# Gate projections as seven half-size products, with the latents and q put ahead of the attention loop

## The chip, the cores and the metric

The kernel runs on one core of a Trainium2 chip. The metric is the device time of one execution in microseconds (us). The time before is the median of three runs. A profile of one execution shows which engine ran which instruction when: PE (TensorE, matmuls; PEld its weight loads), DVE (VectorE), ACT (ScalarE), POOL (GpSimd), and SP, whose queue issues DMAs. Each engine works through its instructions in the order in which the program holds them, and waits there for what the next one needs.

## What is computed

One decoder block for 1024 rows of 1024 fp32 values, with two attentions side by side whose outputs are gated and added, and a SwiGLU:

```python
h = rmsnorm(x, mix_norm_g[l])
proj = h @ w_in[l]
qa, ka, va, q_lat, kv_lat, k_r, g_a, g_b = jnp.split(proj, IN_OFFSETS, axis=-1)
o_a = swa_sink_attention(rope(qa), rope(ka), va, swa_sinks[l])      # window 128, 8 heads of 64
cq = rmsnorm(q_lat, q_norm_g[l]);  qb = cq @ w_uq[l]                # 384 wide
ckv = rmsnorm(kv_lat, kv_norm_g[l]);  kvb = ckv @ w_ukv[l]          # 256 wide
o_b = mla_attention(qb, kvb, rope(k_r))                             # causal, 8 heads
y = sigmoid(g_a) * (o_a @ w_o_swa[l]) + sigmoid(g_b) * (o_b @ w_o_mla[l])
x = x + y @ w_out[l]
h = rmsnorm(x, ffn_norm_g[l])
x = x + (silu(h @ w_gate[l]) * (h @ w_up[l])) @ w_down[l]
return rmsnorm(x, final_norm_g)
```

The gates `g_a` and `g_b` are the last 2048 columns of `proj`: a product of 1024 x 1024 with 1024 x 2048.

## The kernel before

Every fp32 operand of a product is split into a high part (a cast on ACT, line 151) and a low part (a subtraction on DVE, line 152), and `mm3` forms a product as three matmuls: high by high (158), high by low (159), low by high (160). A matmul works on 128 x 128 weights and up to 512 columns. h stands transposed in SBUF in four quarters (`quad`: half of the inner dimension by half of the rows), each with its hh and hl.

The stages follow one another: the normalisation of x with its transposes `tp` and the projection `kvq` (k, v and the first half of q, eight blocks of 128 rows); the loop of the windowed attention; the latents; the second attention (MLA); the two output projections `oA` and `oB`, gated as they come; `xo` (w_out); the FFN; the down projection; the last norm. The FFN and the down projection are already done by Strassen's scheme: of two by two blocks, seven products instead of eight, at the price of sums of weight blocks on POOL (line 893, 896), of `h` blocks (the sets t1 to t4), and of sums of outputs on DVE (`pu`, `u`).

The loop (lines 545 to 567) has 16 iterations, one for each block and group of heads. An iteration transposes q (`qT`), splits it (`qs`), forms the scores (`sc`), adds the mask and takes the maximum (DVE, lines 467 and 469), forms -max (`nm`), the exponentials (ACT, `pe`), the sink's part (`es`), the denominator (`den`, which waits for ACT) and its reciprocal; POOL scales `pe` (line 484); the next iteration transposes it (`pT`), splits it (`pth`, `ptl`), multiplies by v (`o`) and adds the halves into `oa`. Between these steps stand the four steps of one `Gate` unit: 48 matmuls of 128 x 512, 12 a step, that need nothing from the softmax. Every unit has 128 output columns of the gates for all rows, its weights (8 x 128 columns) are loaded and split through the `Stream`, and its result goes by ACT copies (`go`) to DRAM (`gate_d`), from where the output projections read it back. In the second eight iterations `sw_q` also projects the other half of q (`qa`, lines 433 to 436).

After the loop the latents are projected block by block (`ql`, `kl`), normed, transposed (`lT`) and split into `cq` and `ckv`, while the next block's projection runs.

SBUF is managed in two pools of equal slots: U (4 KB a partition, 26 slots) and V (8 KB, 14 slots). A tile waits for a free slot of its pool. A scheduler sets each engine's order from the order of the code and the dependencies.

## Time and profile before

| | us |
|---|---|
| median of three runs | 1420.12 (1419.7 to 1422.82) |
| the profiled execution | 1420.83 |
| its span, first to last instruction | 1419.0 |
| stages, about: start and kvq | 0 to 72 |
| loop with the gates | 72 to 330 |
| latents | 330 to 400 |
| MLA | 400 to 580 |
| output projections, gating | 580 to 700 |
| w_out and the start of the FFN | 700 to 800 |
| FFN | 800 to 1205 |
| down projection, last norm | 1205 to 1419 |

A line of a group reads: source line, engine, operation, output <- inputs, shapes, count | busy us, mean ns of one | idle us of the engine just before them, and what ended that idle time. A line of the timeline reads: start, duration, engine, line, operation, operands, and in brackets the idle time ahead and what ended it. A busy PE is one with a matmul in flight; consecutive matmuls overlap.

### The profile page before, as it was taken

How to read it: one execution, taken by the hardware profiler on the slowest of the kernel's cores; microseconds unless marked ns; L12 is line 12 of the kernel's file. 1: busy time of each engine (PE TensorE's matmuls, PEld its weight loads, DVE VectorE, ACT ScalarE, POOL GpSimd, SP SyncE). 2: the span in 40 equal slices, each digit the busy share in tenths (PEclk: the TensorE clock that was granted, in tenths of full speed). 3: DMA queues.
4: the chain of work that ended last, by engine and by line, in shares of the span. 5: the costliest groups of instructions: out<-in, count | busy, mean ns of one | idle time of the engine just before them, and what ended most of it. 6: DMA issues, size and time to landing. Idle time of an engine off the chain costs nothing. (4 is left out here: it accounts for less than half of the span.)

```text
span 1419.0 us, 18767 instructions
## 1 busy us (share of the span) xinstructions
PE 1377.1 (97%) x6808; PEld 1154.1 (81%) x6808; DVE 875.8 (62%) x1438; ACT 597.4 (42%) x1202; POOL 446.9 (31%) x408
## 2 busy tenths in 40 slices
PE   6999999999999999999997899999999999999997
PEld 5888788889988888878786688888888888888885
DVE  5754644554578776457348766576666666555556
ACT  4345433352467777546135323222332233534252
POOL 1001101111124346122005755586555552010300
PEclk9999999999999999999998999999999999999999
DMA  5223221231000001357135255555445446956543
GB/s 204 75 60 109 69 90 48 96 97 53 24 1 9 10 29 47 120 173 242 45 140 165 75 171 170 178 190 168 152 143 169 150 156 237 361 187 203 160 157 134
DMA packets 129100, 179.82 MB, mean 127 GB/s; under 512 B 8944, under 2 KB 81648, under 8 KB 129008
## 3 DMA queue, kind: packets, MB, share of 16 engines
q1 hardware_dynamic: 126704, 170.23, 36.5%
q10 hardware_dynamic: 2304, 8.39, 1.5%
q8 instruction: 54, 0.88, 0.3%
q14 instruction: 38, 0.31, 0.1%
HBM read 128.00 MB, written 50.59 MB: 126 GB/s over the span
## 5 line engine op out<-in xcount | busy, mean ns | idle before, releaser
L152 DVE TENSOR_TENSOR wl<-wr,wl 128x512 fp32r<-128x512 f32 x132 | 146.5, 1130 | 37.8 <-ACT wl L151 34.3
L152 DVE TENSOR_TENSOR lrl<-lr,lrh 128x1024 fp32r<-128x1024 f32 x77 | 100.1, 1330 | 45.8 <-ACT lrh L151 40.0
L159 PE MATMUL fd<-lrl,lrh 128*128 128x512 f32 x308 | 120.1, 390 | 1.9 <-DVE lrl L152 1.9
L160 PE MATMUL fd<-lrh,lrl 128*128 128x512 f32 x308 | 119.9, 389 | 0.0
L158 PE MATMUL fd<-lrh 128*128 128x512 f32 x308 | 119.0, 389 | 0.0
L151 ACT CAST lrh<-lr 128x1024 fp32r<-128x1024 f32 x77 | 78.4, 1051 | 73.2 <-DVE lrl L152 33.2
L484 POOL TENSOR_SCALAR pe<-pe,den 128x256 f32<-128x256 f32 (+1 forms) x64 | 30.9, 502 | 233.3 <-ACT es L480 103.2
L158 PE MATMUL g<-hh,wh 128*128 128x512 f32 x256 | 101.6, 397 | 0.0
L159 PE MATMUL g<-hl,wh 128*128 128x512 f32 x256 | 100.1, 391 | 0.0
L160 PE MATMUL g<-hh,wl 128*128 128x512 f32 x256 | 99.9, 390 | 0.0
L293 POOL TENSOR_TENSOR rstd<-ms,neg_half 128x1 f32<-128x1 f32 x39 | 21.5, 550 | 240.9 <-DVE ms L291 189.5
L151 ACT CAST wl<-wr 128x512 fp32r<-128x512 f32 x132 | 75.5, 619 | 42.1 <-POOL wr L893 42.1
L708 POOL TENSOR_SCALAR p<-p,denb 128x384 f32<-128x384 f32 (+3 forms) x64 | 49.3, 775 | 106.3 <-DVE denb L707 76.7
L159 PEld LDWEIGHTS fd<-lrl,lrh 128*128 128x128 f32 x308 | 57.8, 188 | 14.6 <-DVE lrl L152 2.7
L158 PEld LDWEIGHTS fd<-lrh 128*128 128x128 f32 x308 | 57.8, 188 | 12.1
L160 PEld LDWEIGHTS fd<-lrh,lrl 128*128 128x128 f32 x308 | 57.8, 188 | 12.0
L152 DVE TENSOR_TENSOR wl<-wr,wh 128x1024 fp32r<-128x1024 f32 (+1 forms) x48 | 58.3, 1219 | 12.5 <-ACT wh L151 11.6
L706 ACT ACTIVATE p<-scb,nmb 128x384 f32<-128x384 f32 (+3 forms) x64 | 47.7, 746 | 37.0 <-DVE nmb L703 33.6
L703 DVE TENSOR_REDUCE nmb<-scb 128x1 f32<-128x384 f32 (+3 forms) x64 | 48.1, 751 | 14.0 <-PE scb L701 13.4
L160 PEld LDWEIGHTS g<-hh,wl 128*128 128x128 f32 x256 | 48.1, 188 | 10.3
L152 DVE TENSOR_TENSOR ptl<-pTb,pth 128x512 fp32r<-128x512 f32 (+2 forms) x96 | 49.7, 549 | 9.3 <-ACT pth L151 8.5
L158 PEld LDWEIGHTS g<-hh,wh 128*128 128x128 f32 x256 | 48.2, 188 | 8.9
(304 smaller groups left out, 4015.0 us busy)
## 6 DMA issues: line engine op xcount, KB each, us to landing
lr<-la_d SPq DMA_DIRECT2D x77, 256.0 KB, 4.2
wr<-in_w_gate_dram SPq DMA_DIRECT2D x44, 256.0 KB, 5.1
wr<-in_w_up_dram SPq DMA_DIRECT2D x44, 256.0 KB, 4.9
wd<-in_w_down_dram SPq DMA_DIRECT2D x22, 512.0 KB, 5.5
rb_d<-wd SPq DMA_DIRECT2D x22, 512.0 KB, 2.9
la_d<-sd SPq DMA_DIRECT2D x22, 512.0 KB, 3.1
lr<-rb_d SPq DMA_DIRECT2D x44, 256.0 KB, 3.7
wr<-in_w_in_dram SPq DMA_DIRECT2D x20, 512.0 KB, 3.9
```

Of the source, the lines that this page charges most:

```text
L151: nc.scalar.copy(hi, src)
L152: (eng or nc.vector).tensor_tensor(lo, src, hi.bitcast(F32), op=ALU.subtract)
L158: nc.tensor.matmul(ps, ah, bh, start=first and i == 0, stop=False, skip_group_check=go_on)
L159: nc.tensor.matmul(ps, ah, bl, start=False, stop=False, skip_group_check=go_on)
L160: nc.tensor.matmul(ps, al, bh, start=False, stop=last and i == n - 1, skip_group_check=go_on)
L293: nc.gpsimd.tensor_tensor(r, ms, neg_half, op=ALU.pow)
L484: nc.gpsimd.tensor_scalar(pe[:, h, c0:], pe[:, h, c0:], den[:, h:h + 1], 0.0, op0=ALU.mult, op1=ALU.add)
L703: nc.vector.tensor_reduce(nm, sc[:, 0:w], axis=AX.X, op=ALU.max, negate=True)
L706: nc.scalar.activation(p[:, 0:w], sc[:, 0:w], AF.Exp, bias=nm, accum_out=den)
L708: nc.gpsimd.tensor_scalar(p[:, 0:w], p[:, 0:w], den, 0.0, op0=ALU.mult, op1=ALU.add)
```

## The change

The gates become an instance of a new class `Seven`, which the FFN uses as well: for each of 8 pairs of 128 columns (j and j + 8) seven products of 12 matmuls, 128 x 512 each, half the inner dimension by half the rows. A product's weights are prepared (`prep`) four products ahead: loads of two 256 KB halves a pair, for product 6 and 7 four POOL operations, and for each product a split `wl` of 128 x 512. `run` issues the matmuls and what is done with their output: product 1 is copied by ACT (`pu`), product 2 is copied to `go`, 6, 7, 5, 4 and 3 are added out of PSUM by DVE. Each result is stored by SP as 256 KB (32 stores) where ACT stored 512 KB (16).

To have the t sets of h ready for the gates, and the slots for them, other columns of `w_in` come first: `kvq`, then `qa` for all blocks, then the latents `ql` and `kl` (blocks 4 to 7 first). q of both groups goes to DRAM (`q_d`) and each iteration loads its own; the normed latents go to DRAM (`lat_d`) and are loaded again after the loop, where they are transposed. While the latents are projected, `sets_of_h` builds t1 to t4 from the quarters. An iteration of the loop now has three products (36 matmuls) in place of 48 gate matmuls; two more products follow it, and six stand among the `lT` transposes and after them. U has 21 slots, V 17; the weights of `kvq`, w_out, the keys of MLA, the FFN (from its second pair on) and the down operands take V slots, and the down stage loads and converts one unit further ahead.

```diff
-U_SLOTS = 26
-V_SLOTS = 14
+LAT = QL + KVL + 2 * ROPE_B
+HF = NF // 2
+U_SLOTS = 21
+V_SLOTS = 17
...
+    def halves_of(shape, wide):
+        if wide:
+            t = V("wv", F32R, (P, 2) + shape[1:])
+            return t[:, 0], t[:, 1]
+        return U("wh", F32R, shape), U("wl", F32R, shape)
...
+            hi, lo = halves_of(shape, wide)
...
+    def plain(key, src, shape, wide=False):
+        joined(key, [(src, shape[-1])], shape, wide)
...
+    def rope_q(ps, g, b):
+        qn = U("qn")
+        rope_nat(halves(ps, 32), 4, 32, rope_a[:, 0, b], rope_a[:, 1, b], [halves(qn[:, 0:256], 32)])
+        nc.sync.dma_start(q_d[g * NB + b], qn[:, 0:256])
...
+    wqa = [st.get(("qa", j)) for j in range(2)]
+    for b in range(NB):
+        ps = PX("qa", (P, 256))
+        mm3(ps, [(hT(k, blk(b)), (wqa[k // 4][0][:, k % 4], wqa[k // 4][1][:, k % 4])) for k in range(NK)])
+        rope_q(ps, 1, b)
...
+    def whole(dst, pair, c):
+        hi, lo = pair
+        add(dst, hi[:, :, blk(c)].bitcast(F32), lo[:, :, blk(c)].bitcast(F32), nc.gpsimd)
+    t4_raw = []
+    def sets_of_h(c):
+        if c == 0:
+            for name in ("t2", "t3", "t1"):
+                new_h(name)
+        r = U("hr", F32, (P, 2, 4, P))
+        t = U("ht", F32, (P, 2, 4, P))
+        whole(r[:, 0], quad[(0, 0)], c)
+        whole(t[:, 0], quad[(0, 1)], c)
+        whole(t[:, 1], quad[(1, 1)], c)
+        whole(r[:, 1], quad[(1, 0)], c)
+        sub(r[:, 0], t[:, 0], r[:, 0], nc.vector)
+        sub(t[:, 0], t[:, 1], t[:, 0], nc.gpsimd)
+        sub(t[:, 1], t[:, 1], r[:, 0], nc.vector)
+        sub(r[:, 1], r[:, 1], t[:, 1], nc.gpsimd)
+        split_h("t2", c, t[:, 1])
+        split_h("t3", c, t[:, 0])
+        split_h("t1", c, r[:, 0])
+        t4_raw.append(r)
...
+    for i, b in enumerate((4, 5, 6, 7, 0, 1, 2, 3)):
+        t = U("lat", F32, (P, LAT))
+        ps = PX("ql", (P, 416))
+        mm3(ps, [(hT(k, blk(b)), (wql[k // 2][0][:, k % 2], wql[k // 2][1][:, k % 2])) for k in range(NK)])
+        latent_norm(t[:, 0:QL], ps, QL, qg_bc)
...
+        latent_norm(t[:, QL:QL + KVL], ps, KVL, kvg_bc)
+        nc.sync.dma_start(lat_d[b], t)
+        if i < 4:
+            sets_of_h(i)
+    for nm, q in (("b11", (0, 0)), ("b21", (1, 0)), ("b22", (1, 1))):
+        hq[nm] = quad.pop(q)
...
+    B_OF = {1: "b11", 2: "b21", 3: "b22", 4: "t4", 5: "t1", 6: "t2", 7: "t3"}
+    ORDER = (1, 6, 2, 7, 5, 4, 3)
+    class Seven:
...
+        NEEDS = {1: (0,), 2: (1,), 6: (0, 1), 7: (0, 1), 5: (), 4: (1,), 3: (1,)}
...
+        def prep(self, j, q, m):
+            i, last = self.ms.index(m), m == self.ms[-1]
+            a = {}
+            for kh in self.NEEDS[q]:
+                self.load_part(j, kh)
+                for f in range(2):
+                    a[(kh, f)] = self.raws[(j, kh)][m][:, :, f]
+            if q == 6:
+                if i == 0:
+                    self.s1[j] = U("s1", F32, (P, 2, 4, P))
+                s = self.s1[j][:, i]
+                add(s, a[(0, 1)], a[(1, 1)], nc.gpsimd)
+                sub(a[(0, 1)], a[(0, 0)], a[(0, 1)], nc.gpsimd)
+                sub(a[(0, 0)], s, a[(0, 0)], nc.gpsimd)
+            if q == 7:
+                sub(a[(1, 0)], a[(1, 0)], a[(0, 0)], nc.gpsimd)
+            src = self.s1[j][:, i] if q == 5 else a[{1: (0, 0), 2: (1, 0), 6: (0, 0), 7: (0, 1), 4: (1, 1), 3: (1, 0)}[q]]
+            t = U("wl", F32R, (P, 2, 4, P))
+            split(t[:, 0], t[:, 1], src)
+            self.left[(j, q, m)] = t
+            if q == 7 and last:
+                self.raws.pop((j, 0))
+            if q == 3 and last:
+                self.raws.pop((j, 1))
+        def prep_to(self, n):
+            while self.n_prep < min(len(self.seq), n):
+                self.prep(*self.seq[self.n_prep])
+                self.n_prep += 1
...
+        def run(self):
+            j, q, m = self.seq[self.n_run]
+            self.prep_to(self.n_run + self.n_ahead)
+            self.n_run += 1
+            if m == self.ms[0] and j + 1 < self.pairs:
+                for kh in range(2):
+                    if q == self.load_at[kh]:
+                        self.load_part(j + 1, kh)
+            t = self.left.pop((j, q, m))
+            if q in (1, 5):
+                self.acc[("A", m)] = P1("fa")
+            if q == 6:
+                self.acc[("B", m)] = PX("fb")
+            ps = self.acc[("A" if q in (1, 2, 5, 3) else "B", m)]
+            rh, rl = hq[B_OF[q]]
+            mm3(ps, [((t[:, 0, k], t[:, 1, k]), (rh[:, k], rl[:, k])) for k in range(4)], first=q in (1, 6, 5),
+                go_on=q in (2, 7, 4, 3))
+            if q == 1:
+                self.tmp[m] = U("pu", F32, (P, 2, 512))
+            if q == 7:
+                if len(self.ms) == 1:
+                    self.u3 = [self.s1[j][:, 1].rearrange("p k c -> p (k c)")]
+                elif m == self.ms[0]:
+                    t = U("u3", F32, (P, 2, 512))
+                    self.u3 = [t[:, 0], t[:, 1]]
+            p1, u2 = self.tmp[m][:, 0], self.tmp[m][:, 1]
+            if q == 1:
+                nc.scalar.copy(p1, ps)
+            elif q == 6:
+                add(u2, ps, p1, nc.vector)
+            elif q == 7:
+                add(self.u3[self.ms.index(m)], ps, p1, nc.vector)
+            else:
+                u3 = self.u3[self.ms.index(m)] if q == 5 else None
+                self.done(j, m, ps, *{2: (0, 0, None), 5: (1, 1, u3), 4: (1, 0, p1), 3: (0, 1, u2)}[q])
+            return j, q, m
...
+    def load_gate(j, kh):
+        t = U("wr", F32, (P, 4, 2, P))
+        for f in range(2):
+            nc.sync.dma_start(t[:, :, f], w_in_cols(C_GATE + (j + NK * f) * P, P, 4 * kh, 4))
+        return {"g": t}
+    def gate_done(j, m, ps, f, sh, other):
+        key = f ^ sh
+        if (j, key) not in gate_out:
+            gate_out[(j, key)] = U("go", F32, (P, 2, 512))
+        dst = gate_out[(j, key)][:, f]
+        if other is None:
+            nc.scalar.copy(dst, ps)
+        else:
+            add(dst, ps, other, nc.vector)
+        nc.sync.dma_start(gate_d[j + NK * f][:, half(sh)], dst)
+    gates = Seven(NK, "g", load_gate, gate_done, 4, (6, 2))
...
     def sw_q(it):
-        g, b = divmod(it, NB)
-        if g == 0:
-            sw[it] = {"qn": q0[b // 4][:, b % 4]}
-            return
-        psq = P1("qa", (P, 256))
-        mm3(psq, [(hT(k, blk(b)), (wqa[k // 4][0][:, k % 4], wqa[k // 4][1][:, k % 4])) for k in range(NK)])
         qn = U("qn")
-        rope_nat(halves(psq, 32), 4, 32, rope_a[:, 0, b], rope_a[:, 1, b], [halves(qn[:, 0:256], 32)])
+        nc.sync.dma_start(qn[:, 0:256], q_d[it])
         sw[it] = {"qn": qn}
...
-    class Gate:
...
     N_SW = 2 * NB
+    gates.load_part(0, 0)
+    gates.load_part(0, 1)
+    sw_q(0)
+    new_h("t4")
+    for c in range(4):
+        split_h("t4", c, t4_raw.pop(0)[:, 1])
     for it in range(-1, N_SW - 1):
-        gi = it + 1
-        if gi == 6:
-            wqa = [st.get(("qa", j)) for j in range(2)]
-        gt = Gate(gi)
-        st.load_to(st.index[("gate", gi)] + 2)
-        sw_q(it + 1)
-        gt.step()
+        if it + 2 < N_SW:
+            sw_q(it + 2)
+        gates.run()
+        sw_qT(it + 1)
+        gates.run()
         if it >= 0:
             sw_pT(it)
-        sw_qT(it + 1)
-        if gi + 1 < N_SW:
-            st.conv_to(st.index[("gate", gi + 1)])
-            st.load_to(st.index[("gate", gi + 1)] + 1)
-        if gi >= N_SW - 2:
-            st.conv_to(st.index[("ql", 1)] + 2 * (gi - N_SW + 2))
-        gt.step()
+        sw_scores(it + 1)
+        gates.run()
         if it >= 0:
             sw_pv(it)
-        sw_scores(it + 1)
-        gt.step()
-        gt.step()
...
+    sw_pT(N_SW - 1)
+    gates.run()
...
+    lat = []
     for b in range(NB):
...
-        latent_T(tq, cq, b)
...
+        t = U("lat", F32, (P, LAT))
+        nc.sync.dma_start(t, lat_d[b])
+        lat.append(t)
+    cq = [hi_lo("cq") for _ in range(3)]
+    for b in range(4):
+        latent_T(lat[b][:, 0:QL], cq, b)
+    gates.run()
...
+    ffn = Seven(HF, "gu", load_w, ffn_done, 4, (7, 5), (1, 2, 6, 7, 5, 4, 3))
...
-    LOADS, CONVS = 9, 4
+        v = V("lrv", F32R, (P, 2, 2, 512))
+        split(v[:, 0], v[:, 1], t)
+        lr[(q, j)] = (v[:, 0], v[:, 1])
+    LOADS, CONVS = 10, 5
```

The orders below are of single engines.

DVE in the loop, before. The rows are the part of one iteration from the split of the next gate weights to the reciprocal of the denominator (`wl` is the low part of gate weights, 128 x 1024, other names as above):

```order
L152 TENSOR_TENSOR wl_2096<-wr_1877,wh_2095 128x1024
L467 TENSOR_TENSOR sc_2123<-sc_2123,band 128x512
L515 TENSOR_TENSOR oa_1963<-o_2113,ot_2118 64x2x128
L516 TENSOR_TENSOR oa_1963<-o_2113,ot_2118 64x2x128
L469 TENSOR_REDUCE mx_2122<-sc_2123 128x2
L467 TENSOR_TENSOR sc_2130<-sc_2130,band 128x512
L469 TENSOR_REDUCE mx_2122<-sc_2130 128x2
L472 SCALAR_TENSOR_TENSOR nm_2137<-mx_2122,nsink 128x4
L479 TENSOR_TENSOR es_2145<-nm_2137,nsink 128x4
L481 TENSOR_TENSOR den_2139<-den_2139,es_2145 128x4
L482 RECIPROCAL den_2139<-den_2139 128x4
```

DVE in the loop of the changed kernel, from one nm on (`wl` are low parts of gate weights, 128 x 512, `pu` an add of a gate product out of PSUM):

```order
L662 SCALAR_TENSOR_TENSOR nm_2540<-mx_2525,nsink 128x4
L669 TENSOR_TENSOR es_2548<-nm_2540,nsink 128x4
L671 TENSOR_TENSOR den_2542<-den_2542,es_2548 128x4
L672 RECIPROCAL den_2542<-den_2542 128x4
L154 TENSOR_TENSOR wl_2557<-wr_2367,wl_2557 128x512
L705 TENSOR_TENSOR oa_2456<-o_2574,ot_2579 64x2x128
L706 TENSOR_TENSOR oa_2456<-o_2574,ot_2579 64x2x128
L154 TENSOR_TENSOR wl_2586<-wr_2339,wl_2586 128x512
L438 TENSOR_TENSOR pu_2602<-fb_2618,pu_2602 128x512
L638 TENSOR_TENSOR qs_2607<-qT_2604,qs_2607 64x2x128
L639 TENSOR_TENSOR qs_2607<-qT_2604,qs_2607 64x2x128
L154 TENSOR_TENSOR wl_2612<-s_417_2487,wl_2612 128x512
```

One split of 128 x 1024 in an iteration has become three of 128 x 512, and adds out of PSUM (here `pu`) have come between the attention's steps; behind `es` stands `den`, as before.

ACT at the start of the program, before and after (`xn` the square of x for the norm, `hh` the high part of transposed h, `wh` and `wv` casts of the weights of `kvq`):

```order
L151 CAST wh_172<-wr_112 128x1024
L151 CAST wh_176<-wr_115 128x1024
L151 CAST hh_134<-tp_158 128x4x128
L151 CAST wh_180<-wr_123 128x1024
L151 CAST hh_138<-tp_165 128x4x128
L151 CAST wh_184<-wr_126 128x1024
L304 ACTIVATE xn_192,ss_193<-x_129 128x1024
```

The same place in the changed kernel:

```order
L299 ACTIVATE xn_189,ss_190<-x_130 128x1024
L153 CAST hh_136<-tp_159 128x4x128
L299 ACTIVATE xn_197,ss_198<-x_185 128x1024
L153 CAST hh_140<-tp_166 128x4x128
L153 CAST hh_136<-tp_224 128x4x128
L153 CAST hh_140<-tp_231 128x4x128
L153 CAST wv_173<-wr_113 128x1024
```

The weight casts moved behind two squares and four hh casts. On DVE the weights' low parts moved likewise, behind `nsink` and the norms of two blocks.

SP's queue after the loop of the changed kernel (`lat` the latents coming back, `wr` weights, `gate_d` the store of a gate result):

```order
L619 DMA gate_d<-go_3682 128x512 x2
L708 DMA oa_d<-oa_3443 128x1024
L750 DMA lat_3756<-lat_d 128x704
L750 DMA lat_3758<-lat_d 128x704
L750 DMA lat_3760<-lat_d 128x704
L750 DMA lat_3762<-lat_d 128x704
L750 DMA lat_3764<-lat_d 128x704
L750 DMA lat_3766<-lat_d 128x704
L750 DMA lat_3768<-lat_d 128x704
L750 DMA lat_3770<-lat_d 128x704
L240 DMA wr_3892<-in_w_uq_dram 128x3x192
```

The loads of the latents, which the program before did not have, stand behind the store of the loop's last `oa`.

More of the change, by code (lines that the diff above doesn't have):

```diff
@@ new lines, in add, with new_h, split_h @@
+    def add(out, a, b, eng):
+        eng.tensor_tensor(out, a, b, op=ALU.add)
+    hq = {}
+    def new_h(name):
+        hq[name] = (V(name + "h", F32R), V(name + "l", F32R))
+    def split_h(name, c, src, eng=None):
+        hi, lo = hq[name]
+        split(hi[:, :, blk(c)], lo[:, :, blk(c)], src, eng)
+    def whole(dst, pair, c):
[20 more added lines that the diff above has]
+        t4_raw.append(r)
@@ L578, in hybrid_block_kernel @@
-    nc.gpsimd.tensor_copy(causal_b, band[:, P:2 * P])
-    make_identity(nc, ident_b)
-    wql = [st.get(("ql", j)) for j in range(4)]
-    wkl = [st.get(("kl", j)) for j in range(2)]
+    sw_pT(N_SW - 1)
+    gates.run()
+    sw_pv(N_SW - 1)
+    gates.run()
     def hi_lo(name):
@@ L657, in hybrid_block_kernel @@
     prod_q(0, 1)
-    latent_T(tk, ckv, NB - 1)
-    for s in range(2):
-        pr = P1("krT", (HD, 4, P))
-        for j in range(4):
-            nc.tensor.transpose(pr[:, j], kr_all[:, 4 * s + j].rearrange("p u d -> p (u d)"), ident)
-        for hi, lo in kT:
-            split(hi[64:128, half(s)], lo[64:128, half(s)], pr.rearrange("p b c -> p (b c)"))
     def prod_v(b):
```

312 lines of the change are left out of this document (111 added, 201 removed).

## The prediction

> **What bounds the kernel now.** I start with the busy times of the page, and then ask whether TensorE's share is real.
>
> ```profile
> span 1419.0 us, 18767 instructions
> ...
> PE 1377.1 (97%) x6808; PEld 1154.1 (81%) x6808; DVE 875.8 (62%) x1438; ACT 597.4 (42%) x1202; POOL 446.9 (31%) x408
> ...
> PE 40%; DVE 2%; POOL 2%; issue 1%; ACT 0%; DMA 0%; DVEq 0%; POOLq 0%; SPq 0%; ACTq 0%
> ...
> L158 PE MATMUL g<-hh,wh 128*128 128x512 f32 x256 | 101.6, 397 | 0.0
> ```
>
> PE leads, and it leads the chain that ended last (third line). But the 397 ns of one gate matmul are not its price. The timeline of one gate stretch has these two matmuls with 18 others between them:
>
> ```profile
> 133.29 0.39 PE L158 MATMUL g<-hh,wh 128*128 128x512 f32 x1
> ...
> 137.60 0.39 PE L159 MATMUL g<-hl,wh 128*128 128x512 f32 x1
> ```
>
> From 133.29 to 137.60 are 19 steps: 4.31/19 = **0.227 us** from start to start. Each overlaps the next, so a matmul taken from a full stretch is worth 0.227, not 0.397. The windows say which stretches are full (after the times: busy PE, PEld, DVE, ACT, POOL, then clock, DMA share, GB/s):
>
> ```profile
> 200.00:264.00 64.00, 64.00 (x353) 55.48 (x352) 34.16 (x75) 25.67 (x67) 5.72 (x13) 1.00 0.20 63
> ...
> 375.00:400.00 25.00, 24.63 (x129) 20.34 (x128) 19.51 (x47) 15.98 (x38) 4.96 (x6) 1.00 0.05 12
> ...
> 750.00:775.00 25.00, 18.31 (x81) 14.63 (x80) 19.98 (x26) 12.74 (x23) 16.33 (x14) 0.89 0.42 142
> 775.00:800.00 25.00, 20.43 (x71) 14.62 (x71) 21.18 (x21) 11.21 (x19) 19.95 (x13) 0.84 0.25 81
> ...
> 850.00:1000.00 150.00, 150.00 (x664) 124.24 (x663) 99.85 (x113) 44.43 (x80) 95.98 (x67) 1.00 0.54 176
> ```
>
> The loop that holds the gates (200 to 264 is a part of it) never lets PE go, and DVE is busy for 34 of its 64 us. So work taken from PE there is time won, until DVE becomes the one to wait for. PE stands idle at the very start and from 750 to 800, ahead of the FFN.
>
> **What goes.** 768 gate matmuls become 8 x 7 x 12 = 672: 96 x 0.227 = **-21.8 us**. (By their durations it would be 38; the steps in the timeline exclude that.)
>
> **The loop.** Its DVE rows, from the groups of the window 75 to 330:
>
> ```profile
> L467 DVE TENSOR_TENSOR sc<-sc,band 128x512 f32<-128x512 f32 (+1 forms) x32 | 20.9, 661 | 11.2 <-PE sc L466 11.1
> L469 DVE TENSOR_REDUCE mx<-sc 128x2 f32<-128x512 f32 (+1 forms) x32 | 20.8, 657 | 0.9
> L152 DVE TENSOR_TENSOR ptl<-pT,pth 128x512 fp32r<-128x512 f32 x30 | 19.4, 686 | 44.4 <-ACT pth L151 44.4
> L449 DVE TENSOR_TENSOR qs<-qT,qs 64x256 fp32r<-64x256 f32 x15 | 6.4, 427 | 0.5
> ...
> L516 DVE TENSOR_TENSOR oa<-o,ot 64x256 f32<-64x256 f32 x15 | 6.3, 418 | 0.2
> ...
> L482 DVE RECIPROCAL den<-den 128x4 f32<-128x4 f32 x16 | 2.9, 178 | 0.5
> L481 DVE TENSOR_TENSOR den<-den,es 128x4 f32<-128x4 f32 x16 | 2.6, 163 | 29.2 <-ACT es L480 29.2
> L479 DVE TENSOR_TENSOR es<-nm,nsink 128x4 f32<-128x4 f32 x16 | 2.6, 163 | 1.0
> L472 DVE SCALAR_TENSOR_TENSOR nm<-mx,nsink 128x4 f32<-128x4 f32 x16 | 2.6, 161 | 0.5
> ```
>
> The timeline gives the period, from one den to the next:
>
> ```profile
> 122.22 0.16 DVE L481 TENSOR_TENSOR den<-den,es 128x4 f32<-128x4 f32 x1 [1.89 <-ACT es L480]
> ...
> 136.12 0.16 DVE L481 TENSOR_TENSOR den<-den,es 128x4 f32<-128x4 f32 x1 [1.89 <-ACT es L480]
> ```
>
> PE: of 136.12 - 122.22 = 13.90 us, 48 x 0.227 = 10.9 are gates, so 3.0 are attention. With three products of 12 matmuls an iteration needs 36 x 0.227 + 3.0 = **11.2 us**.
>
> DVE: the attention's sc, mx, ptl, qs and oa come twice in an iteration, the four small ones once: 2 x (0.661 + 0.657 + 0.686 + 0.427 + 0.418) + 0.665 = 6.36 us. New are three wl splits of 128x512 (0.686 each, like ptl, which has the same shape) and adds out of PSUM: five of seven products end in one, 3 x 5/7 = 2.14 an iteration. The FFN does the same and has their price (groups of the window 800 to 1200, the last line POOL's preparation):
>
> ```profile
> L152 DVE TENSOR_TENSOR wl<-wr,wl 128x512 fp32r<-128x512 f32 x123 | 136.7, 1133 | 35.9 <-ACT wl L151 32.5 <-DMA wr<-in_w_gate_dram 2.0
> L152 DVE TENSOR_TENSOR wl<-s,wl 128x512 fp32r<-128x512 f32 x20 | 30.8, 1577 | 32.0 <-ACT wl L151 32.0
> L896 DVE TENSOR_TENSOR pu<-fb,pu 128x512 f32<-128x512 f32 x42 | 28.6, 683 | 10.5 <-PE fb L160 10.5
> ```
>
> ```profile
> L896 POOL TENSOR_TENSOR s<-wr,wr 128x512 f32<-128x512 f32 x20 | 28.3, 1417 | 58.9 <-DMA wr<-in_w_up_dram 54.1 <-DMA wr<-in_w_gate_dram 4.7
> ```
>
> So 6.36 + 3 x 0.686 + 2.14 x 0.683 = 9.88 us of work. To that comes den's wait for ACT's exponentials, 29.2/16 = 1.83 us. In the order of the changed kernel nothing stands between es and den in most iterations, and one add in four of fifteen, which takes 0.18 off the mean. DVE cannot go round in less than **11.5 us**: it, not PE, would set the loop, for 0.3 x 16 = 5 us. On top come collisions with POOL. A split beside POOL costs up to 1.577 - 0.686 = 0.89 more, and POOL gets 8 x 4 preparations of 1.4 us, 45 of the loop's 185 us. 48 splits x 45/185 x 0.89, halved for partial overlap, is 5; I take 4, since a preparation must end before the splits that read it begin. Loop **+9**. Its bounds: 0, if adds filled all waits of den, and 5 + 48 x (1.133 - 0.686) = 26, if splits cost as in the FFN. While DVE waits at den, or at an add for its product, the next splits, qs and ptl queue behind it; the products split ahead are the cover that keeps PE fed, and where they run out each us of DVE is one of PE. The adds' outputs, 32 stores of 256 KB on SP's queue instead of 16 on ACT's, and q's 16 stores and loads (asked for two iterations ahead) lie beside a DMA share of 0.20: nothing; a late q would hold a transpose and the whole softmax behind it.
>
> **The start.** Rows of the timeline; the last is the final matmul of the second block's projection:
>
> ```profile
> 9.09 1.97 PE L313 MATMUL tp<-ident,xn 128*128 128x128 f32 x8 [9.09 <-DVE xn L378]
> ...
> 9.65 1.05 ACT L151 CAST wh<-wr 128x1024 fp32r<-128x1024 f32 x1 [4.98 <-DMA wr<-in_w_in_dram]
> ...
> 13.78 1.22 DVE L152 TENSOR_TENSOR wl<-wr,wh 128x1024 fp32r<-128x1024 f32 x1
> ...
> 16.65 0.26 DVE L421 TENSOR_SCALAR nsink<-nsink 128x8 f32<-128x8 f32 x1
> ...
> 17.25 1.06 ACT L304 ACTIVATE xn<-x 128x1024 f32<-128x1024 f32 x1 [1.14 <-DMA x<-in_x_dram]
> ...
> 21.18 1.03 PE L313 MATMUL tp<-ident,xn 128*128 128x128 f32 x8
> ...
> 29.73 0.39 PE L160 MATMUL kvq<-wh,hl 128*128 128x512 f32 x1
> ```
>
> Before, the weight casts stood first on ACT (9.65). Now two squares of x and four hh casts stand ahead of them, the second square waiting for its x (17.25), and on DVE nsink (16.65) stands ahead of every split. Block 1 is then normalised at about 18.9 (0.3 for ms, 0.6 for rstd, 1.3 for xn after nsink) and transposed by 20.9. The wv casts run from 21.6 to 25.8, four of 1.05, the last split ends at 27.5 (four of 1.22 from 22.6), block 0 at 28.3 and block 1 24 matmuls later, at 33.8, against 30.1: **+4** (bounds +1, where an earlier landing lets the casts go sooner, and +8, where PE comes to them at the half speed of the 9.09 row).
>
> **After the loop.** The latents move ahead of the loop, with 16 splits and 8 subtractions for the t sets laid on a DVE that has half its time there: +1 (0 to 4, with the hand-over to the first gate product). But they come back through memory, and SP issues their eight loads only behind the last oa store.
>
> ```profile
> L152 DVE TENSOR_TENSOR cq<-lT,cq 128x128 fp32r<-128x128 f32 x23 | 6.6, 289 | 2.6 <-ACT cq L151 2.5
> ```
>
> ```profile
> oar<-oa_d SPq DMA_DIRECT2D x4, 512.0 KB, 4.1
> ```
>
> A landing of about 4.1 us is covered by the 27 gate matmuls that PE has in between (6.1 us). Then DVE paces it: 40 lT splits x 0.289 = 11.6, six small ones of wuq 1.7, three wl and two wv 3.4, two adds 1.4: 18 us. PE has 48 transposes, at 1.03/8 = 0.13 each 6.2, and 35 gate matmuls, 7.9: 14. That leaves 4, and 1.5 for taking turns, less the 0.4 that 375 to 400 lost before: **+5** (0 to 14; 14 if the loads come one by one and the cover runs out).
>
> **The FFN's start.** In the waits of 700 to 800:
>
> ```profile
> PE tp L912 <- DVE xn L306: 8.6, 7, 3.7
> ```
>
> The last transposes there stood 5 to 24 matmuls apart; now a whole xo product of 24 (5.4 us) lies between most of them, so some of the 8.6 should go: **-2** (-8 to +4). The FFN's steady state, MLA and down keep their work, and PE covers the one subtraction that moves in the FFN: 0 (-2 to +2).
>
> **Sum**, against the profiled execution: 1420.8 (span 1419.0 and 1.8 around it; the median of the runs shown is 1420.1) - 21.8 + 9 + 4 + 1 + 5 - 2 = **1416 us**. Three quarters of what goes is given back.
>
> **Rivals.** (a) *PE stays the bound* (20%). The products split ahead ride out den's wait, the loop costs 0 and the tail's splits hide too: 1416 - 9 - 5 = 1402. For it: DVE has 9.88 of work against PE's 11.2. Against: DVE goes in order, and in most iterations nothing stands behind es to fill. (b) *DVE and POOL collide as in the FFN* (20%). The loop costs 26: 1416 + 17 = 1433. It decides from a loop period of 11.2 + (9 + 7)/16 = 12.2 us on; above that the kernel is slower than before. For it: the same operations, 1.133 a split there. Against: POOL is busy for a quarter of the time here, for 96 of 150 us there. (c) *The ends give all back* (8%). The loads after the loop are not covered, and the start costs its 8: 1416 + 4 + 3 = 1423. (d) *POOL shuts DVE out for whole instructions* (2%): each of the 32 preparations costs DVE its 1.417, 45 us in place of the 4: 1457. Against it: the worst row is 0.89 over a lone split. That the matmuls do not go is excluded by their count in the order.
>
> The Trainium skill, "SBUF — State Buffer", section "SBUF: two separate sides", says what (d) would follow: DVE and GpSimd share a pair of ports under an exclusive lock, and whoever comes second blocks for the whole instruction. The rows agree in kind (1.577 against 0.686), not in the full size.
>
> **How the numbers follow.** The forecast has 50% (its own range 1408 to 1424). A measurement of this kernel can tell about 0.2%, 3 us. Faster, below 1417.3: 30 of the forecast's 50, and (a): 0.50. Same: 14 of it and 3 of (c): 0.17. Slower: the other 6, (b), (d) and 5 of (c): 0.33. The range reaches to the middles of (a) and (b) and leaves out their far halves: 1402 to 1434.
>
> **What would show it.** Right: 672 gate matmuls at 0.227; den to den 11.5 to 12 us, with DVE busy for most of the loop and den still waiting for es; wl splits near 0.75; the first kvq near 22 us; some 5 us of PE gaps among the lT transposes. A period of 11.2 without gaps on PE would be (a), over 12.2 with wl over 1.1 (b), gaps of more than 10 us around the loads (c). The forecast falls first with the price of the collisions, next with the tail.

## The result, and the profile after

The changed kernel takes 1471.26 us (median of four runs, 1468.46 to 1473.32), against 1421.47 for the kernel before: a ratio of 1.035, with a 95% interval of 1.032 to 1.037. It is 3.5% slower; the forecast was 1416, and the time lies above its range. The page of the profiled execution, in the lines that were shown of before:

```profile
span 1470.6 us, 19063 instructions
...
PE 1379.7 (94%) x6712; PEld 1146.9 (78%) x6712; DVE 954.0 (65%) x1542; ACT 607.3 (41%) x1242; POOL 538.9 (37%) x464
```

PE has 96 matmuls less, as it should, yet is busy for as long as before (1379.7 against 1377.1): a matmul whose successor comes late, or that runs at half speed, counts for longer. DVE and POOL have 78 and 92 us more. The windows cut at the stages (columns as before: busy PE, PEld, DVE, ACT, POOL, clock, DMA share, GB/s):

```profile
97.00:179.00 82.00, 68.52 (x391) 66.21 (x389) 48.77 (x111) 19.00 (x51) 42.57 (x39) 0.88 0.21 66
179.00:396.00 217.00, 197.07 (x942) 157.90 (x943) 151.75 (x309) 104.12 (x289) 81.10 (x97) 0.97 0.28 87
396.00:421.00 25.00, 20.50 (x106) 15.20 (x105) 18.33 (x60) 14.34 (x56) 0.54 (x1) 1.00 0.65 223
421.00:604.00 183.00, 174.53 (x1096) 148.48 (x1095) 139.00 (x280) 126.43 (x292) 73.15 (x81) 0.99 0.08 25
```

These are the latents, the loop, the stretch with the transposed latents, and MLA. PE, which before filled the loop, is idle in all four, and no other engine is full in any of them: DVE is busy for 152 of the loop's 217 us. So the time went into waits, not into an engine that became the bound. A part of it went into TensorE's clock (the column ahead of the DMA share): 0.88 in 82 us of latents and 0.97 in 217 us of the loop are, as an estimate (82 x 0.12 and 217 x 0.03), 10 and 6.5 us of full clock. The stages, measured in the timelines from the start of a stage's first matmul to the start of the next one's first (kvq, qa, the latents and the loop are counted up to the start of their own last matmul):

| stage | before | after | |
|---|---|---|---|
| start and kvq | 68.4 | 73.8 | +5.4 |
| loop, qa, latents, transposed latents | 311.6 | 347.4 (qa 23.7, latents 80.5, loop 217.0, transposed latents 26.2) | +35.8 |
| MLA, output projections | 283.5 | 290.8 | +7.3 |
| w_out | 99.4 | 97.6 | -1.8 |
| FFN | 435.4 | 440.9 | +5.5 |
| down, last norm | 211.7 and 8.9 | 211.1 and 9.0 | -0.5 |

The second line holds most of it: with 21.8 us of matmuls gone it should be 289.8 us, and is 57.6 longer than that. What PE waits for there, in the latents (97 to 180) and in the loop (180 to 396); a line is the waiting engine and line, what it waited for, us in all, times, longest:

```profile
PE ql L160 <- DVE rp L354: 6.9, 2, 3.9
PE kl L160 <- ACT wh L153: 5.1, 1, 5.1
...
PE sc L655 <- DVE qs L638: 10.6, 3, 5.0
PE pT L686 <- POOL pe L674: 3.0, 6, 0.6
...
DVE den L671 <- ACT es L670: 23.4, 13, 2.0
DVE wl L154 <- ACT wl L153: 21.1, 7, 4.8
...
ACT wl L153 <- POOL wr L435: 27.3, 5, 5.8
```

The last line is new: before, ACT did not wait for POOL at all in this loop. The line ahead of it has grown: before, DVE waited 3.0 us there for the casts of gate weights. The splits themselves, in the groups of DVE from 185 to 395:

```profile
L154 DVE TENSOR_TENSOR wl<-wr,wl 128x512 fp32r<-128x512 f32 x44 | 33.0, 754 | 22.6 <-ACT wl L153 21.1
```

They are short, and DVE stands idle ahead of them for 22.6 us. The timeline of one such wait in the loop, all engines, without the gate matmuls:

```profile
229.13 1.38 POOL L674 TENSOR_SCALAR pe<-pe,den 128x256 f32<-128x256 f32 x3
...
230.29 1.04 PE L686 MATMUL pT<-ident,pe 128*128 128x128 f32 x8
...
230.48 1.26 POOL L438 TENSOR_TENSOR s<-wr,wr 128x512 f32<-128x512 f32 x1
231.82 1.26 POOL L435 TENSOR_TENSOR wr<-wr 128x512 f32<-128x512 f32 x1
233.16 1.26 POOL L435 TENSOR_TENSOR wr<-s,wr 128x512 f32<-128x512 f32 x1
234.45 0.62 ACT L153 CAST wl<-wr 128x512 fp32r<-128x512 f32 x1 [5.76 <-POOL wr L435]
235.09 0.36 ACT L636 CAST qs<-qT 64x256 fp32r<-64x256 f32 x1
235.10 0.69 DVE L154 TENSOR_TENSOR wl<-wr,wl 128x512 fp32r<-128x512 f32 x1 [4.81 <-ACT wl L153]
...
235.87 0.42 DVE L638 TENSOR_TENSOR qs<-qT,qs 64x256 fp32r<-64x256 f32 x1
...
236.34 0.58 PE L655 MATMUL sc<-khd,qs 128*128 128x256 f32 x1 [5.01 <-DVE qs L638]
```

It reads from the bottom up. PE waits 5 us for `qs`. `qs` itself is ready to be split, but on ACT and on DVE it stands behind `wl`, the split of a new pair's product 6, whose weights are a sum of three POOL operations, and POOL began them only when it had scaled the softmax. The split is needed several products later; in an in-order queue its wait is everybody's. Den to den, the fifteen periods of the loop are 11.2, 12.1, 11.7, **16.5, 14.0, 15.0**, 12.2, 10.7, 11.2, 12.1, **16.5, 13.2, 15.7**, 12.2, 11.7: nine are about what was forecast, six are not.

### The profile page after: what moved, and what is told of

Read it like the earlier page. It is cut to its first block, busy times and chain, and to the rows that moved or that the text cites. A ratio compares the mean times of both kernels' runs of the same rounds, so it can differ in the third digit from the quotient of the medians.

```text
span 1470.6 us, 19063 instructions
## 1 busy us (share of the span) xinstructions
PE 1379.7 (94%) x6712; PEld 1146.9 (78%) x6712; DVE 954.0 (65%) x1542; ACT 607.3 (41%) x1242; POOL 538.9 (37%) x464
## 5 line engine op out<-in xcount | busy, mean ns | idle before, releaser
L154 DVE TENSOR_TENSOR wl<-wr,wl 128x512 fp32r<-128x512 f32 x180 | 189.6, 1073 | 111.7 <-ACT wl L153 108.6
L153 ACT CAST wl<-wr 128x512 fp32r<-128x512 f32 x180 | 105.1, 621 | 160.8 <-POOL wr L435 157.6
L154 DVE TENSOR_TENSOR lrv<-lr,lrv 128x1024 fp32r<-128x1024 f32 x77 | 101.4, 1352 | 56.6 <-ACT lrv L153 51.9
L153 ACT CAST lrv<-lr 128x1024 fp32r<-128x1024 f32 x77 | 80.0, 1053 | 105.6 <-PE fd L162 56.1
L288 POOL TENSOR_TENSOR rstd<-ms,neg_half 128x1 f32<-128x1 f32 x39 | 23.5, 603 | 265.3 <-DVE ms L286 217.0
L161 PE MATMUL fd<-lrv 128*128 128x512 f32 x308 | 119.9, 389 | 0.8 <-DVE lrv L154 0.8
L160 PE MATMUL fd<-lrv 128*128 128x512 f32 x308 | 119.8, 389 | 0.6 <-ACT lrv L153 0.6
L162 PE MATMUL fd<-lrv 128*128 128x512 f32 x308 | 119.8, 389 | 0.0
L435 POOL TENSOR_TENSOR wr<-wr,wr 128x512 f32<-128x512 f32 x30 | 43.1, 1438 | 78.3 <-DVE wl L154 61.9
L161 PEld LDWEIGHTS fd<-lrv 128*128 128x128 f32 x308 | 57.8, 188 | 13.1 <-DVE lrv L154 1.1
L160 PEld LDWEIGHTS fd<-lrv 128*128 128x128 f32 x308 | 57.8, 188 | 12.9 <-ACT lrv L153 1.0
L162 PEld LDWEIGHTS fd<-lrv 128*128 128x128 f32 x308 | 57.8, 188 | 11.9
L435 POOL TENSOR_TENSOR wd<-wd 128x512 f32<-128x512 f32 x22 | 33.1, 1504 | 84.6 <-DMA wd<-in_w_down_dram 84.4
L154 DVE TENSOR_TENSOR ptl<-pTb,pth 128x512 fp32r<-128x512 f32 (+2 forms) x96 | 50.2, 549 | 13.3 <-ACT pth L153 13.2
L666 ACT ACTIVATE pe<-sc,nm 128x256 f32<-128x256 f32 (+1 forms) x64 | 28.6, 459 | 69.3 <-DVE nm L662 64.7
L162 PE MATMUL fb<-t2h,wl 128*128 128x512 f32 x120 | 47.6, 397 | 2.4 <-DVE wl L154 2.4
```

Source lines behind the costliest of these rows:

```text
L153: nc.scalar.copy(hi, src)
L154: (eng or nc.vector).tensor_tensor(lo, src, hi.bitcast(F32), op=ALU.subtract)
L160: nc.tensor.matmul(ps, ah, bh, start=first and i == 0, stop=False, skip_group_check=go_on)
L161: nc.tensor.matmul(ps, ah, bl, start=False, stop=False, skip_group_check=go_on)
L162: nc.tensor.matmul(ps, al, bh, start=False, stop=last and i == n - 1, skip_group_check=go_on)
L288: nc.gpsimd.tensor_tensor(r, ms, neg_half, op=ALU.pow)
```

## The experiments

All run beside the kernel before, one time each unless a ratio is given; times of single runs are compared by their stages. How far a stage moves by itself is seen where its code is the same: the stretch from MLA to the mix took 288.9 to 290.8 us in eleven runs, the FFN 440.5 to 447.3.

**Three places alone, and one undone.** The weights of kl, asked for earlier:

```diff
             st.load_to(st.index[("ql", b)])
+        if b in (5, 6):
+            st.load_to(st.index[("kl", b - 5)])
```

> The weights of kl are asked for while q's second half is projected, not after it; nothing else changes. In the trace of the change PE waits 5.05 us for their casts (kl <- ACT wh) and then runs some 3 us at half speed. Theory (a late load): that wait goes, the latents shorten by 5 to 7 us, total about 1465. Rival (DVE and POOL, busy with the t sets, set the pace of the latents): the wait comes back at the next block, total 1470 to 1471.

1460.44 us; the latents fell from 80.5 to 73.4. The trace of the change shows why:

```profile
100.52 0.93 SPq L207 DMA_DIRECT2D wr<-in_w_in_dram  x2
106.27 1.04 ACT L153 CAST wh<-wr 128x1024 fp32r<-128x1024 f32 x1 [12.76 <-DMA wr<-in_w_in_dram]
107.37 0.58 PE L160 MATMUL kl<-wh,hh 128*128 128x256 f32 x1 [5.05 <-ACT wh L153]
```

SP issues that load only at 100.52, behind the last stores of q and three loads of constants. A late load, then; it cost 7 us.

The t sets moved whole into q's part:

```diff
         rope_q(ps, 1, b)
+        if b in (1, 3, 5, 7):
+            sets_of_h((1, 3, 5, 7).index(b))
...
-        if i < 4:
-            sets_of_h(i)
```

> The four calls that build t1 to t4 move from the first four latent blocks to blocks 1, 3, 5 and 7 of q's second half. Theory (their POOL and DVE work stands ahead of the latents' norms, which hold the PSUM banks that PE waits for): the waits of ql for DVE in the latents (6.9 us, and the half clock behind them) go, q's part has room for them, total 1457 to 1463. Rival (the two engines have too much work, wherever it stands): the same waits come up in q's part, total 1468 to 1471.

1486.46 us, the other way: the latents took 86.5, q's part 26.1. Neither expectation held. PE's waits between 73 and 186:

```profile
PE ql L161 <- DVE wl L154: 17.0, 2, 10.4
PE kl L160 <- ACT wh L153: 4.5, 1, 4.5
```

Now the splits of ql's weights stand on DVE behind the t sets, which themselves go in turns with POOL. Where the work stands in the queue matters, and at the new place it stood ahead of something that was needed sooner.

The POOL sums of product 6 made two products earlier, the last one into a buffer of its own:

```diff
-                add(s, a[(0, 1)], a[(1, 1)], nc.gpsimd)
-                sub(a[(0, 1)], a[(0, 0)], a[(0, 1)], nc.gpsimd)
-                sub(a[(0, 0)], s, a[(0, 0)], nc.gpsimd)
...
+            add(s, a[(0, 1)], a[(1, 1)], nc.gpsimd)
+            sub(a[(0, 1)], a[(0, 0)], a[(0, 1)], nc.gpsimd)
+            if len(self.ms) == 1:
+                sub(self.s1[j][:, 1], s, a[(0, 0)], nc.gpsimd)
...
+            if len(self.ms) == 1 and self.n_run > 0:
+                for jj, qq, m in self.seq[self.n_prep:n + 2]:
+                    if qq == 6:
+                        self.sums(jj, m)
```

> In the loop the three POOL sums that product 6 of a pair needs are made two products earlier, the last of them into a buffer of its own, so that none waits for the split of product 1; same work. Theory (ACT, then DVE, wait in order for POOL: wl <- POOL wr, 27.3 us in five waits, and qs and the softmax stand behind): the long periods of 13 to 16.5 us from den to den shrink to 11.5 to 12.5, loop 12 to 20 us shorter, total 1451 to 1459. Rival (DVE's work, or its port shared with POOL, sets the period): no period changes by more than 1 us, total 1468 to 1473.

1456.01 us, the loop 203.3 in place of 217.0. The longest period is 13.8, the mean 12.1 in place of 13.1. The waits of the loop in that run:

```profile
DVE den L693 <- ACT es L692: 22.9, 13, 2.0
DVE wl L154 <- ACT wl L153: 5.5, 4, 4.5
...
ACT wl L153 <- POOL s L435: 5.3, 1, 5.3
```

27.3 us of ACT's waits for POOL became 5.3. The work is the same, so it was the place of the sums, not their amount; whether the earlier place or the buffer of its own did more was not tried. The gain has two parts: PE's idle time in the loop fell from some 20 to 11 us, and the granted clock rose from 0.97 to 1.00. Three periods (13.8, 13.1, 12.8) stay above the expected 12.5.

The weights of the first projection back in U slots (`True` taken away from `joined(("x1", j), ...)`), so that their casts stand first on ACT:

> The weights of the first projection take U slots again, as before the change; the casts then stand first on ACT. Theory (the order at the start, +5.5 us by the trace): the first projection ends 5 us sooner, total about 1466. Rival (the start is covered by what follows, or the four V slots are missed elsewhere): total 1470 or more.

1469.13 us: the start fell from 73.8 to 68.8, about as before the change, but the loop and the stretch behind it took 4.2 us more. In that stretch PE idled as long as in the change, at a clock of 0.88 in place of 1.00. The step is right for its place; the total of this single run lies within those of the change.

**Together, and what is left.** Three edits at once (sums three products early):

> Three edits together: kl's weights asked for early, product 6's POOL sums three products early and out of place, the first projection's weights in U slots. If the three losses are separate places, the gains add (stages: start 69, latents 73, loop 203 or less, total 1438 to 1445). If they are one queue of work that only moves, the total stays above 1450.

1448.2 us, between the two. By stages the gains add (start 68.0, latents 72.1, loop 203.2); the stretch behind the loop took 30.1, 4 us more than in the change, at a clock of 0.89 in place of 1.00.

The t sets in five steps, spread:

```diff
+        if stage == 0:
+            whole(r[:, 0], quad[(0, 0)], c)
+            whole(t[:, 0], quad[(0, 1)], c)
+        elif stage == 1:
...
+PLAN = {('qa', 5): [(0, 0), (1, 0)], ('qa', 6): [(2, 0)], ('qa', 7): [(3, 0)], ('ql', 0): [(4, 0)],
+        ('kl', 0): [(0, 1)], ('ql', 1): [(1, 1), (2, 1)], ..., ('kl', 6): [(4, 3)]}
```

> The three edits, and the work for t1 to t4 cut into five steps a block (two sums, two sums, three differences, one difference and one split, two splits), spread from block 5 of q's second half to latent block 6. Theory (in the latents PE waits for the norms because they stand behind POOL's and DVE's long turn for a t set): the latents fall from 73 to 66 to 69 us against the three edits alone. Rival (the amount of that work, not how it stands in the order, is the cost): latents 72 or more, or the loss appears in q's part.

1435.37 us; the latents fell from 72.1 to 61.2, more than expected, q's part stayed at 23.7, and the loop took 3 us more. The windows of the latents, of e5_three and of e6_pipe:

```profile
91.70:163.80 72.10, 62.05 (x386) 60.36 (x385) 49.24 (x108) 17.90 (x48) 40.78 (x39) 0.98 0.17 58
```

```profile
91.20:152.40 61.20, 59.75 (x386) 58.96 (x385) 45.27 (x108) 18.97 (x49) 34.31 (x34) 1.00 0.17 60
```

PE has the same 386 matmuls, now with 1.5 us idle in place of 10. The work of DVE and POOL is the same, a part of it now standing in q's part. In one turn a t set held up the latents' norms behind it, and the norms held the PSUM banks in which PE wanted to write the next block: PE's waits for `rp` and `lat` of DVE, 5.5 and 4.6 us in e5_three, are gone. A slowing of DVE by POOL is not the reason: the 24 sums and splits of t sets on DVE took 24.3 us in e5_three and 23.7 here, where 24 lone ones of 0.69 would take 16.6.

The denominator by POOL, so that DVE no longer waits for the exponentials:

```diff
-        nc.vector.tensor_tensor(den, den, es, op=ALU.add)
-        nc.vector.reciprocal(den, den)
+        nc.gpsimd.tensor_tensor(den, den, es, op=ALU.add)
+        nc.gpsimd.tensor_tensor(den, den, neg_one, op=ALU.pow)
```

> The three edits, and the softmax's denominator (es added, reciprocal) made by POOL instead of DVE, so that DVE no longer waits for ACT's exponentials in each iteration (22.9 us in 13 waits). Theory of the prediction (DVE's 9.9 us of work and 1.8 us of wait set the loop): periods den to den fall from 12 to 11.2 to 11.6, the loop by 6 to 12 us. Rival (the wait of den is slack, the period comes from PE's work and single waits for POOL): loop within 3 us of the three edits alone, or longer, since POOL's two small operations come into the chain ahead of pT.

1454.19 us, the loop 205.8 against 203.2. With DVE's 23 us of waiting gone the loop is not shorter. Either the wait was slack, or it was worth no more than the two small POOL operations cost that now stand in the chain; this run cannot tell the two apart.

Two of three sums of product 6 earlier in the FFN too (the `for` above without its condition on `ms`):

> The three edits, and in the FFN too two of the three POOL sums of product 6 are made two products earlier. Theory (FFN +5 us: PE waits once a pair, 0.5 to 0.7 us, for the split of product 6, which waits for POOL): the FFN falls from 441 to about 436. Rival (the new class loads a pair's weights too late): no change, or longer.

1449.13 us, the FFN 443.6 against 441.8: no gain beyond the scatter. What the FFN lost is not explained by this.

pT with one more product between the scores and it, and v's product behind that:

```diff
         gates.run()
+        if it >= 1:
+            sw_pv(it - 1)
         sw_qT(it + 1)
+        gates.run()
+        sw_scores(it + 1)
         gates.run()
         if it >= 0:
             sw_pT(it)
-        sw_scores(it + 1)
-        gates.run()
-        if it >= 0:
-            sw_pv(it)
+    gates.run()
+    sw_pv(N_SW - 2)
     sw_pT(N_SW - 1)
     gates.run()
     sw_pv(N_SW - 1)
-    gates.run()
```

> On top of e6_pipe: in the loop pT of an iteration comes after its successor's scores and one more product, and the product with v after that; same instructions. Theory (what is left in the loop, 12.1 us a period against 11.2 of PE's work, is the way from the scores to pT, some 9 us through DVE, ACT and POOL, which three products hardly cover): with four products in between the periods fall to 11.2 to 11.7, the loop by 5 to 12 us. Rival (DVE's work sets 11.5 to 12): loop within 3 us of 206.

1435.83 us, the loop 211.2 against 206.3. Ten of fifteen periods are 10.5 to 11.9, about PE's 11.2, which speaks for the theory; but the other five, 13.1 to 15.1, make the loop longer, which neither side foresaw. PE's longest waits in it are for a copy of a gate product by ACT (4.2 us in two) and for `wl` (6.6 us in five).

Three loads of the latents asked for in the last three iterations:

```diff
+        if it >= N_SW - 4:
+            load_lat(it - N_SW + 4)
...
+    for b in range(3, NB):
+        load_lat(b)
```

> On top of e6_pipe: three of the eight loads of the latents are asked for during the last three iterations, not after them. Theory (the tail is set by DVE's splits of lT, as predicted): tail within 2 us of 27.7. Rival (by the landing of the loads): tail 4 us shorter or more.

1428.95 us; the stretch fell from 27.7 to 23.3. Not all of that is the landing. The clock over the stretch is 0.94 in e6_pipe, 1.00 here and 1.00 in the change, where the stretch took 26.2: at equal clock the three loads give 2.9 us. In f1_all below, the same edit at a clock of 0.93 gave 26.0, 1.7 less than e6_pipe. So the landing counts, for 2 to 3 us, and the rest is the clock.

The split attention output back in U slots (`halves_of((P, 2, 512), False)` in `split_oa`):

> On top of e6_pipe: the split windowed-attention output that waits for the mix takes U slots again, as before the change. Theory (the 6.3 us for which PE waits at the end of MLA come from casts of that output that the new slots let stand ahead of the last probabilities on ACT): the stage from MLA to the mix falls from 289 to 284 to 286. Rival (it comes from the order of qT or of the weights): 288 or more.

1436.13 us; MLA to the mix fell from 289.4 to 285.2, and in f1_all it is 285.3. PE's longest wait there, of the change and of this run (before the change it was 1.7):

```profile
PE ob L886 <- DVE ptl L154: 6.3, 1, 6.3
```

```profile
PE ob L923 <- DVE ptl L154: 2.1, 1, 2.1
```

The timeline of the change, all engines, only the rows of the outputs and of the probabilities:

```profile
594.54 2.18 ACT L153 CAST wv<-oar 128x512 fp32r<-128x512 f32 x4
...
595.72 4.97 POOL L154 TENSOR_TENSOR wv<-oar,wv 128x512 fp32r<-128x512 f32 x4
...
597.28 4.57 DVE L154 TENSOR_TENSOR obT<-ob,obT 128x512 fp32r<-128x512 f32 x2 [1.19 <-ACT obT L153]
...
602.90 1.47 DVE L154 TENSOR_TENSOR ptl<-pTb,pth 128x512 fp32r<-128x512 f32 x3
```

Four casts of that output stand on ACT, their low parts fill POOL for 5 us, and beside these two splits on DVE take 4.57 us; the probabilities for which PE waits come after them.

All of these together:

> e6_pipe with the edits of e10_lat and e11_oa together. If the places are separate, their gains add (4.4 in the tail, 4.2 in MLA): total 1425 to 1429, still slower than before by 0.3 to 0.8%, because the loop keeps some 14 us of its own waits. A total at 1432 or above would say that the waits move on.

1426.97 us (1426.24 to 1430.5), a ratio of 1.005 to before (95%: 1.003 to 1.007). The edits give back 44 of the 50 us lost, and the kernel is still no faster than before: half a per cent slower, less than the 2% from which a time is called different here. The sum came out as expected, the parts less so: against e6_pipe the stretch behind the loop gave 1.7 and MLA to the mix 4.1, and small changes elsewhere the rest. The loop, in the windows:

```profile
152.00:358.00 206.00, 191.48 (x939) 154.35 (x939) 153.29 (x312) 104.53 (x289) 83.31 (x96) 0.99 0.33 101
```

Against the loop of the change, PE is idle for 14.5 us in place of 19.9, and it is busy for 5.6 us less with as many matmuls, at a clock of 0.99 in place of 0.97.

Three tries at the 12.1 us a period that are left: two of four heads scaled by ACT (the diff), products split five ahead (the 4 in `Seven(NK, "g", load_gate, gate_done, 4, (6, 2))` becomes 5), and e9_pT's order with the sums four products early (`n + 4`):

```diff
+            if h >= 2:
+                nc.scalar.activation(pe[:, h, c0:], pe[:, h, c0:], AF.Copy, scale=den[:, h:h + 1])
+                continue
```

> f1_all with two of the four heads of pe scaled by ACT instead of POOL. Theory (the way from the scores to pT, 9 us over DVE, ACT and POOL, sets what is left of the loop, POOL's four scalings being 2.4 of it): PE's waits for pe shrink and the loop falls by 5 to 12 us, total 1414 to 1421. Rival (DVE's 11.5 us): loop within 3 us of f1_all.

> f1_all with the weights of a gate product split five products ahead, not four. If what is left of the loop comes from splits that are not ready, it falls by 3 us or more; by the theory of the way from the scores to pT it stays within 2 us.

> f1_all with pT after four products instead of three (as e9_pT) and product 6's POOL sums four products early, not three. In e9_pT plain periods fell to 11.3 to 11.6 and those with a new pair's sums rose to 13 to 15. If the latter come from POOL's sums, they fall below 12.5 here and the loop to 192 to 200; if from PSUM banks that wait for a copy by ACT, they stay.

All were slower than f1_all: 1435.41 us (ratio to before 1.011, 1.009 to 1.013; loop 214.0), 1446.43 (loop 220.8) and 1439.74 (loop 216.7). So none of the three theories brought its gain. In f3_five the long periods are 15 to 19 us, and ACT waits for POOL's sums only once, for 5.5 us, as in f1_all; what makes them long was not found. In f4_late the long periods stayed (13 to 18 us) although the sums came earlier, which by the expectation speaks for PSUM banks, but PE's waits for a copy by ACT are 4.3 us in two and do not explain all of it. What the remaining 0.9 us a period come from is open: in f1_all's loop PE's longest waits are 4.6 us for `wl` and 4.3 for `pe`, and each edit that shortens one lengthens another.

## Why the prediction was wrong

- **What goes, -21.8.** Right in the count, 96 matmuls less, and in the step: gate matmuls in the loop of the change still stand 0.23 us apart where PE does not wait.
- **The loop, +9.** This is the first step that failed: the mean period is 13.1 us against PE's 11.2, some 30 us over 16 iterations where I had 9. The term for collisions was right in size: the wl splits of the loop took 754 ns on the mean, 0.07 more than a lone one, 3 to 4 us for 48 where 4 stood. But "DVE cannot go round in less than **11.5 us**: it, not PE, would set the loop" is not what held: DVE is busy for 152 of 217 us, and three of the fifteen periods are shorter than that (11.2, 10.7, 11.2). That nine periods came out near 11.5 is luck, as far as the runs show, and does not save the reason. What the step left out is POOL's sums as a wait: I priced the 32 preparations by what they cost DVE at the port, and never asked when they are ready. In the sentence on what queues behind a waiting instruction I named DVE's wait at den and at the adds, not ACT's wait for POOL. The waits of the kernel before had the row, in its FFN, which works by the same scheme:

```profile
ACT wl L151 <- POOL wr L893: 42.1, 21, 5.0
```

The late sums cost 13.7 us of the loop (e3_sums), the slow stretches of the clock behind the long waits included.

- **The latents, +1.** The second step that failed, by some 18 us. I laid the 16 splits and 8 differences on "a DVE that has half its time there", an argument by busy share. e6_pipe shows with the same work that the place in the order decides: as one turn a block they cost 10.9 us, in five steps next to nothing. The other 7.1 are a load behind q's stores and three constants on SP (e1_kl). I had counted what the new place in SP's queue does to the latents' loads after the loop, and not what it does to the weights of kl ahead of it. Also, I priced DVE's slowing by POOL for the loop alone, and it is stronger here: of these 24 operations nine took 1.37 to 1.78 us.
- **The start, +4.** Right in place and size (+5.4, the first kvq matmul at 22.4 us), worked out from the two orders; e4_x1 gives it back.
- **After the loop, +5.** PE's gaps are of that size, 4.5 us, and mostly for DVE's splits, as worked out. But "A landing of about 4.1 us is covered" was not right in full: three loads asked for early bring 2 to 3 us (e10_lat, f1_all).
- **MLA and the output projections, 0.** Wrong by 7.3 (by 5.4 to 6.3 in the other runs of this code). These stages "keep their work", but the slots changed their order on ACT; 4.2 come back with e11_oa. I had looked at the orders of the gates' own stages alone.
- **The FFN's start -2, its steady state 0.** The first is right: w_out ended 1.8 sooner, and the FFN's first pairs cost no more than before. Two transposes at its start still wait, 3.2 and 3.5 us. The steady state is wrong: from its fourth pair on the FFN loses some 0.8 us a pair against the kernel before, 5.5 in all. ACT's waits for POOL's sums grew there from 42.1 to 130.3 us, but e8_ffn, which makes two of three sums earlier, gave nothing back, and the cause is open.
- **The rivals.** (a) is excluded by PE's 20 us of idle time in the loop. (b) named POOL and DVE together and had the direction right, slower, but by the port; at 754 ns a split it is excluded as the cause. (c) fails as well: the ends, start and landing, cost 5.4 and 2 to 3 us, and most of the loss lies between them. (d), at the price that it had, is excluded by the same 754; that POOL can hold DVE for more than one whole instruction is shown below, in another stage.

## What to carry to other kernels

Freed matmuls are worth their time only if what is put in their place is ready: for each operation that is new in an in-order queue ask when its input is ready and what stands behind it, and not only what it costs. A busy share of a half says nothing of a long turn: work that has time should be cut into steps that fit between those that something waits for, and sums of operands belong several products ahead of their split, into a buffer of their own. And a change of slot sizes moves the order of stages whose code it does not touch, so compare the orders there as well.

## What was not expected of the hardware

After a long wait PE paid twice. In the latents of the change, matmuls of 416 columns ran at steps of 0.35 us for 5 us after a stop, where 0.19 is usual there:

```profile
138.78 0.35 PE L162 MATMUL ql<-wh,hl 128*128 128x416 f32 x1
138.97 0.35 PE L160 MATMUL ql<-wh,hh 128*128 128x416 f32 x1
...
147.03 0.68 PE L160 MATMUL ql<-wh,hh 128*128 128x416 f32 x1 [3.90 <-DVE rp L354]
147.51 0.55 PE L161 MATMUL ql<-wl,hh 128*128 128x416 f32 x1
...
152.01 0.55 PE L162 MATMUL ql<-wh,hl 128*128 128x416 f32 x1
```

The step from 138.78 to 138.97 is 0.19; from 147.51 to 152.01 thirteen steps are 4.50, 0.35 each. The windows show it as a clock of 0.88 in the latents. The Trainium skill, "TensorE: Matmul & The Clock Gate", Part 1, has it so: an idle window of about 3.4 us halves the clock, and about as long a busy one restores it; here the wait was 3.90 and the slow stretch over 4.5 us.

But so long a wait is not needed. These are two windows of e6_pipe, in the stretch behind the loop:

```profile
378.20:381.60 3.40, 1.38 (x6) 0.86 (x7) 3.37 (x16) 3.40 (x12) 0.00 (x0) 1.00 0.26 107
381.60:385.00 3.40, 3.40 (x10) 2.62 (x9) 2.64 (x6) 0.27 (x2) 0.00 (x0) 0.50 0.00 0
```

In the first PE is busy for 1.38 of 3.40 us, a few transposes at a time, and its longest wait is 1.07 us. In the second the clock is 0.50. So short gaps that leave PE mostly idle for some 3.4 us had the same effect there; what share is enough, these runs do not show. This slow stretch is what makes the 0.94 of e6_pipe above; e10_lat has none.

POOL and DVE do shut each other out. Of the two `obT` splits of the rows above, the first has nearly all the time:

```profile
597.28 3.97 DVE L154 TENSOR_TENSOR obT<-ob,obT 128x512 fp32r<-128x512 f32 x1 [1.19 <-ACT obT L153]
```

A split alone takes 0.69, and the second one took 0.68. The first ended 0.6 us after the last of POOL's four, which stand there without a gap, 1.24 us each. The Trainium skill, "SBUF — State Buffer", section "SBUF: two separate sides", says that the later of the two blocks for the whole instruction. The trace agrees in kind and goes further: the split began during POOL's second operation and came through only when the fourth was done. In the loop this is rare, with the longest wl split at 1.66 us and the mean at 0.754; POOL is busy for 81 of 217 us there.
